# A decoder layer on one core: high weights times high and low activations in one product of 512 columns

## The chip, the cores and the metric

The kernel runs on one core of one Trainium2 chip. The metric is the device time of one execution in microseconds (us); lower is better. The engines are named as in the profile: PE is TensorE (PEld its loads of weights), DVE is VectorE, ACT is ScalarE, POOL is GpSimd, SP is SyncE, which issues the large loads.

## The reference

One layer of a decoder on 256 tokens (S), width 2048 (D), all in float32. Cut to what matters:

```
u = RMSNorm(h)
[qkv_A | z_A | b_A | a_A | q_B | k_B | v_B | g_B | gate_A | gate_B] = u @ w_in     # 2048 x 16400
o_A = gated DeltaNet (short causal conv and silu on q, k, v; chunked delta rule)
o_B = multi-scale retention (rotary q, k; fixed decay per head)
h = h + (sigmoid(gate_A) * o_A + sigmoid(gate_B) * o_B) @ w_out                    # 2048 x 2048
h = h + (silu(hn @ w_gate) * (hn @ w_up)) @ w_down,   hn = RMSNorm(h)              # inner width 5632
return RMSNorm(h)
```

Some 300 MB of weights are read once, each time against 256 tokens.

## The kernel before, in words

**Three passes.** Every product with weights is made of three: each weight tile is rounded to a high part (ScalarE, line 163) and the rest is its low part (VectorE, line 164). The activations are kept in the same two parts, `uh`, `ul` in the first phase, `m` (high and low halves) for the output projection, `hh`, `hl` and `fh`, `fl` behind it. Summed are high weights by high activations (L229), high weights by low activations (L230), and low weights by high activations (L232).

**Units.** The work on weights is a row of units of up to 1 MB. `run_units` takes them one after the other: it emits the load of a unit ahead (SP, L150), the split of a unit ahead, the unit's products, and then what reads the sums (events, `after`). There are three kinds:

- feature-major units (`feature_major`): one tile of 128 output features. The weights are the stationary operand, 128 x 128 for each k-tile, and the 256 tokens of an activation tile move past them. The sums take 256 of the 512 columns of one PSUM bank. With 16 k-tiles that is 48 products of 256 columns; the units of the down projection have 11 k-tiles, so 33. They serve q, k, v of both mixers (`conv_unit`, `rot_evac`; tiles ps_k, ps_q, ps_v, ps_r), the output projection (ps_wo), gate and up (ps_wg, ps_wu) and down (ps_wd).
- token-major units (`token_major`; tiles ps_t): activations stationary, weights moving, 24 products of 512 columns.
- units of Strassen's products (`strassen`; tiles pst_t, pst_sg, pst_su): 21 products of 256 columns of a pair of k-tiles, after VectorE has made three sums of the raw weights (L181 to L183).

**Order.** The first phase (projections and mixers, four blocks of two heads) is ordered by the framework's scheduler on every engine. In the second phase (output projection, gate, up, down) Strassen's units are spread among the others (`FPOS`), and from the 30th unit on (`MAN0`) VectorE keeps the order of the program: split of the unit two ahead, then what reads the sums of the unit before. The other engines stay with the scheduler. Every engine works its own queue in order. High and low parts have two buffers each in the first phase and three in the second, so a split two units ahead waits until TensorE has left a buffer.

**Readers of the sums.** `conv_unit` reads the bank once (L461), `rot_evac` three times (L758 to L760), `wo_evac` (L1071) and `down_ev` (L1176) once, adding to the residual hT; `gate_ev` (L1155) and `up_ev` (L1166) once, multiplying by the norm.

Of the kernel before, what the change touches and what calls it, by code (L numbers as in the profile page):

```python
# [12 lines left out]
P = 128  # L13
# [19 lines left out]
# and where: after which unit of their block, among how many units  # L33
# [15 lines left out]
# buffers; units split ahead in the two phases; units loaded ahead of that  # L49
# [14 lines left out]
def kernel(  # L64
# [15 lines left out]
    # the banks of Strassen's sums serve the units and the mixers as well while there are none  # L80
# [74 lines left out]
    split_ins = {}  # unit -> the last instructions of its split, on ScalarE and VectorE  # L155
# [11 lines left out]
    def load_next(pieces=1):  # L167
        """emit the next unit's split into high and low parts, and its load if that hasn't been"""
# [16 lines left out]
    def after(n, fn):  # L185
        """emit fn after the products of n more units"""
        events.setdefault(done[0] + n, []).append(fn)

    def chain(gen):
        """emit the steps of gen one by one, one after each unit"""  # L190
# [30 lines left out]
    def feature_major(src, nk, ah, al, name, evac):  # L221
        o = []

        def begin():
            o.append(ps_unit(f"ps_{name}")[:, :S])

        def products(hi, lo, k0, k1):
            for k in range(k0, k1):
                PE.matmul(o[0], hi[:, k * P:(k + 1) * P], ah[:, k, :], start=(k == 0), stop=False)  # L229
                PE.matmul(o[0], hi[:, k * P:(k + 1) * P], al[:, k, :], start=False, stop=False)  # L230
            for k in range(k0, k1):
                PE.matmul(o[0], lo[:, k * P:(k + 1) * P], ah[:, k, :], start=False, stop=(k == nk - 1))  # L232
# [10 lines left out]
    def start_pair(before):  # L243
        """the first two units, loaded and computed by quarters in turn, each after what `before` emits"""
# [48 lines left out]
    # -- Strassen's products on one block of 512 columns, token-major --  # L293
    def strassen(src, x, zt, name, then, before=None):
# [3 lines left out]
        def lhs(h):  # L298
# [5 lines left out]
            # product: its token operand, slot of its weights, bank and half of its sum  # L304
# [1046 lines left out]
```

## Time and profile before

| | |
|---|---|
| times of three runs | 1665.67, 1666.42, 1667.9 us; median 1666.42 us |
| span of the profiled execution, first to last instruction | 1664.6 us |
| TensorE | busy 1640.4 us, 13210 products, mean granted clock 0.995 of full speed |
| VectorE | busy 1267.8 us (76%) |
| ScalarE | busy 808.6 us (49%) |
| HBM | 297.27 MB read, 180 GB/s over the span |

The profiled execution is one of the program on the chip; its span leaves out what lies before the first and behind the last instruction, 1.8 us against the median. The records of products overlap (each shows some 160 ns longer than its turn takes), so their pitch, from start to start, is the number to read, not their duration.

### The profile page before, as it was taken

To read this page: it belongs to the slowest core of one execution; us is meant where nothing else is said; L and a number is where in the kernel's file an instruction comes from. 1 tells how busy PE (TensorE), PEld (TensorE's weight loads), DVE (VectorE), ACT (ScalarE), POOL (GpSimd) and SP (SyncE) were. 2 spreads that over 40 slices of the span, in tenths; PEclk is the share of its full clock that TensorE was granted. 3 is DMA by queue.
4 is the path that set the end of the run, shared out by engine and by line. 5 is a ranking of instruction groups with operands and counts; after the bars stand their busy time and mean duration, and the time that the engine had idled before them with its cause. 6 is when DMAs were issued, how large, how long until landed. Compare 5 with 4: busy or idle time off the path is not lost.

```text
span 1664.6 us, 30825 instructions
## 1 busy us (share of the span) xinstructions
PE 1640.4 (99%) x13210; PEld 1558.5 (94%) x13210; DVE 1267.8 (76%) x1719; ACT 808.6 (49%) x850; POOL 28.7 (2%) x63
## 2 busy tenths in 40 slices
PE   7999999999999999999999999999999999999997
PEld 6987899988998889988899999999999999999997
DVE  7797468887888878776675757788778888788754
ACT  5664444445544545445465434444444445354443
POOL 0000000000000000000000000000000000000000
PEclk9999999999999999999999999999999999999998
DMA  7544453454635555344675445465545656466552
GB/s 268 177 153 174 155 194 127 168 185 170 213 131 179 185 180 194 132 168 157 232 270 182 178 152 178 146 219 203 193 170 183 205 190 226 143 205 212 177 181 86
DMA packets 55721, 301.36 MB, mean 181 GB/s; under 512 B 6816, under 2 KB 7072, under 8 KB 32672
## 3 DMA queue, kind: packets, MB, share of 16 engines
q1 hardware_dynamic: 54144, 295.31, 51.4%
q10 hardware_dynamic: 1440, 4.08, 0.7%
q8 instruction: 103, 1.69, 0.4%
q14 instruction: 34, 0.28, 0.0%
HBM read 297.27 MB, written 2.10 MB: 180 GB/s over the span
## 4 chain that ended last, share of the span: by engine, by line
PE 52%; issue 44%; DMA 2%; DVE 2%; ACT 0%; SPq 0%; POOLq 0%; POOL 0%; DVEq 0%; ACTq 0%
PE ps_t L280 7%; PE ps_t L285 7%; PE ps_t L281 7%; PE pst_t L322 6%; PE ps_v L230 2%; PE ps_v L229 2%; PE ps_r L229 2%; PE ps_v L232 2%; PE ps_r L230 2%; PE ps_r L232 2%; PE ps_wo L229 2%; PE ps_wo L230 2%; PE ps_wo L232 1%; PE ps_q L232 1%; PE ps_q L230 1%
## 5 line engine op out<-in xcount | busy, mean ns | idle before, releaser
L163 ACT ACTIVATE hi_t<-raw_t 128x2048 fp32r<-128x2048 f32 (+1 forms) x100 | 183.1, 1832 | 203.7 <-PE ps_t L281 99.2
L164 DVE TENSOR_TENSOR lo_t<-raw_t,hi_t 128x2048 fp32r<-128x2048 f32 (+1 forms) x100 | 217.8, 2182 | 62.4 <-ACT hi_t L163 42.4
L280 PE MATMUL ps_t<-hi_t,uh 128*128 128x512 f32 x480 | 190.7, 397 | 0.5 <-DVE gs L834 0.5
L281 PE MATMUL ps_t<-hi_t,ul 128*128 128x512 f32 x480 | 188.6, 393 | 0.0
L229 PE MATMUL ps_wd<-fh,hi_wd 128*128 128x256 f32 x704 | 169.3, 281 | 1.0 <-DVE fl L1143 1.0
L230 PE MATMUL ps_wd<-fl,hi_wd 128*128 128x256 f32 x704 | 169.6, 281 | 0.0
L229 PEld LDWEIGHTS ps_wd<-fh,hi_wd 128*128 128x128 f32 x704 | 132.8, 189 | 1.2 <-DVE fl L1143 1.2
L230 PEld LDWEIGHTS ps_wd<-fl,hi_wd 128*128 128x128 f32 x704 | 132.9, 189 | 0.0
L163 ACT ACTIVATE hi_wd<-raw_wd 128x1408 fp32r<-128x1408 f32 x64 | 88.4, 1381 | 86.7 <-PE ps_wd L230 35.0
L285 PE MATMUL ps_t<-lo_t,uh 128*128 128x512 f32 x480 | 123.5, 395 | 0.0
L229 PE MATMUL ps_wu<-hh,hi_wu 128*128 128x256 f32 x448 | 109.2, 282 | 0.0
L230 PE MATMUL ps_wu<-hl,hi_wu 128*128 128x256 f32 x448 | 109.1, 283 | 0.0
L230 PE MATMUL ps_wg<-hl,hi_wg 128*128 128x256 f32 x448 | 108.9, 283 | 0.0
L229 PE MATMUL ps_wg<-hh,hi_wg 128*128 128x256 f32 x448 | 108.9, 282 | 0.0
L164 DVE TENSOR_TENSOR lo_wd<-raw_wd,hi_wd 128x1408 fp32r<-128x1408 f32 x64 | 103.6, 1620 | 6.6 <-ACT hi_wd L163 6.5
L280 PEld LDWEIGHTS ps_t<-hi_t,uh 128*128 128x128 f32 x480 | 90.2, 188 | 19.1 <-PE pst_t L322 0.9
L281 PEld LDWEIGHTS ps_t<-hi_t,ul 128*128 128x128 f32 x480 | 90.2, 188 | 17.7
L285 PEld LDWEIGHTS ps_t<-lo_t,uh 128*128 128x128 f32 x480 | 88.9, 188 | 18.1
L232 PE MATMUL ps_wd<-fh,lo_wd 128*128 128x256 f32 x704 | 93.6, 281 | 0.0
L163 ACT ACTIVATE hi_sg<-raw_sg 128x1792 fp32r<-128x1792 f32 x32 | 54.5, 1704 | 71.9 <-DVE raw_sg L183 24.1
L232 PEld LDWEIGHTS ps_wd<-fh,lo_wd 128*128 128x128 f32 x704 | 87.8, 189 | 0.0
L229 PEld LDWEIGHTS ps_wg<-hh,hi_wg 128*128 128x128 f32 x448 | 85.4, 191 | 0.0
(361 smaller groups left out, 4092.1 us busy)
## 6 DMA issues: line engine op xcount, KB each, us to landing
raw_t<-in_wtm_dram SPq DMA_DIRECT2D x60, 1024.0 KB, 4.8
raw_wd<-in_wdown_dram SPq DMA_DIRECT2D x64, 704.0 KB, 4.1
raw_wg<-in_wgate_dram SPq DMA_DIRECT2D x28, 1024.0 KB, 4.8
raw_wu<-in_wup_dram SPq DMA_DIRECT2D x28, 1024.0 KB, 4.8
raw_t<-in_wsm_dram SPq DMA_DIRECT2D x40, 512.0 KB, 3.3
raw_v<-in_wqk_dram SPq DMA_DIRECT2D x16, 1024.0 KB, 4.7
raw_r<-in_wqk_dram SPq DMA_DIRECT2D x16, 1024.0 KB, 4.8
raw_wo<-in_wout_dram SPq DMA_DIRECT2D x16, 1024.0 KB, 4.8
```

Source lines behind the costliest of these rows:

```text
L163: ia = A_.activation(hi[:, r], w[:, r], AF.Copy)
L164: iv = V.tensor_tensor(out=lo[:, r], in0=w[:, r], in1=hi[:, r].bitcast(F32), op=ALU.subtract)
L229: PE.matmul(o[0], hi[:, k * P:(k + 1) * P], ah[:, k, :], start=(k == 0), stop=False)
L230: PE.matmul(o[0], hi[:, k * P:(k + 1) * P], al[:, k, :], start=False, stop=False)
L232: PE.matmul(o[0], lo[:, k * P:(k + 1) * P], ah[:, k, :], start=False, stop=(k == nk - 1))
L280: PE.matmul(pst[c], uh[:, k, c * P:(c + 1) * P], w, start=(k == 0), stop=False)
L281: PE.matmul(pst[c], ul[:, k, c * P:(c + 1) * P], w, start=False, stop=False)
L285: PE.matmul(pst[c], uh[:, k, c * P:(c + 1) * P], lo[:, j * 512:(j + 1) * 512], start=False, stop=(k == KT - 1))
L322: PE.matmul(T[bank][:, half * S:(half + 1) * S], op(j), w[:, slot * 256:(slot + 1) * 256], start=(j == 0 and w is hi and h and half == 0), ...
```

## The change

The two parts of every activation that feature-major units use now lie side by side: `u2`, `h2`, `f2` and `m` are [128, k, 2, 256], and the old names are views of them. For a high weight tile one product of 512 columns takes the place of two of 256: high by high into the first half of the bank, high by low into the second. Low weights by high activations stay products of 256 columns into the first half. The two halves of the bank are added by those who read them.

```diff
         def begin():
-            o.append(ps_unit(f"ps_{name}")[:, :S])
+            o.append(ps_unit(f"ps_{name}"))
 
         def products(hi, lo, k0, k1):
             for k in range(k0, k1):
-                PE.matmul(o[0], hi[:, k * P:(k + 1) * P], ah[:, k, :], start=(k == 0), stop=False)
-                PE.matmul(o[0], hi[:, k * P:(k + 1) * P], al[:, k, :], start=False, stop=False)
+                PE.matmul(o[0], hi[:, k * P:(k + 1) * P], flat(a[:, k]), start=(k == 0), stop=(k == nk - 1),
+                          skip_group_check=True)
             for k in range(k0, k1):
-                PE.matmul(o[0], lo[:, k * P:(k + 1) * P], ah[:, k, :], start=False, stop=(k == nk - 1))
+                PE.matmul(o[0][:, :S], lo[:, k * P:(k + 1) * P], a[:, k, 0], start=False, stop=(k == nk - 1),
+                          skip_group_check=True)
...
-    uh = act.tile([P, KT, S], F32R, tag="a0", name="uh")
-    ul = act.tile([P, KT, S], F32R, tag="a1", name="ul")
+    u2 = act.tile([P, KT, 2, S], F32R, tag="a0", name="u2")
+    uh, ul = u2[:, :, 0], u2[:, :, 1]
...
-            V.tensor_tensor(out=cb[:, 3:], in0=o, in1=rstd_b, op=ALU.mult)
+            cl = t1(f"cl_{name}")
+            A_.activation(cl, o[:, S:], AF.Copy)
+            V.tensor_tensor(out=cl, in0=o[:, :S], in1=cl, op=ALU.add)
+            V.tensor_tensor(out=cb[:, 3:], in0=cl, in1=rstd_b, op=ALU.mult)
...
-            def evac(o):
+            def evac(ps):
+                o = t1(f"ro_{b}_{i}")
+                A_.activation(o, ps[:, S:], AF.Copy)
+                V.tensor_tensor(out=o, in0=ps[:, :S], in1=o, op=ALU.add)
...
-                V.tensor_tensor(out=hT[:, f], in0=o, in1=hT[:, f], op=ALU.add)
+                for i in range(2):
+                    V.tensor_tensor(out=hT[:, f], in0=o[:, i * S:(i + 1) * S], in1=hT[:, f], op=ALU.add)
...
+        def whole(o, name):
+
+            t = t1(name)
+            A_.activation(t, o[:, S:], AF.Copy)
+            V.tensor_tensor(out=t, in0=o[:, :S], in1=t, op=ALU.add)
+            return t
...
-                gs = pend[f] = t1(f"gs{f}")
-                V.tensor_tensor(out=gs, in0=o, in1=rb2, op=ALU.mult)
+                gs = pend[f] = whole(o, f"gs{f}")
+                V.tensor_tensor(out=gs, in0=gs, in1=rb2, op=ALU.mult)
...
-                us = t1(f"us{f}")
-                V.tensor_tensor(out=us, in0=o, in1=rb2, op=ALU.mult)
+                us = whole(o, f"us{f}")
+                V.tensor_tensor(out=us, in0=us, in1=rb2, op=ALU.mult)
```

The edit of hT is in `wo_evac` and `down_ev` alike. The scheduler orders the changed program anew. Three places show how.

**VectorE, among the first down units** (lo_wd and ps_wd are units of the down projection, raw_su, lo_su and Z_sg, sg_g belong to Strassen's units). Before:

```order
L1176 TENSOR_TENSOR hT<-ps_wd_1_10963,hT 128x256
L1112 SCALAR_TENSOR_TENSOR sg_g_11034<-Z_sg_11027,rt_8323,sg_g_11034 128x512
L164 TENSOR_TENSOR lo_su_0_11041<-raw_su_0_10997,hi_su_0_11040 128x1792
L181 TENSOR_TENSOR raw_su_1_11078<-raw_su_1_11078 128x512
L182 TENSOR_TENSOR raw_su_1_11078<-raw_su_1_11078 128x256
L183 TENSOR_TENSOR raw_su_1_11078<-raw_su_1_11078 128x256
L164 TENSOR_TENSOR lo_wd_4_11084<-raw_wd_4_11038,hi_wd_4_11083 128x1408
```

Now:

```order
L1194 TENSOR_TENSOR hT<-ps_wd_1_9778,hT 128x256 x2
L1129 SCALAR_TENSOR_TENSOR sg_g_9838<-Z_sg_9831,rt_7697,sg_g_9838 128x512
L164 TENSOR_TENSOR lo_su_0_9846<-raw_su_0_9801,hi_su_0_9845 128x1792
L181 TENSOR_TENSOR raw_su_1_9872<-raw_su_1_9872 128x512
L182 TENSOR_TENSOR raw_su_1_9872<-raw_su_1_9872 128x256
L183 TENSOR_TENSOR raw_su_1_9872<-raw_su_1_9872 128x256
L164 TENSOR_TENSOR lo_wd_4_9878<-raw_wd_4_9843,hi_wd_4_9877 128x1408
```

The order stands; each reading of the sums has become two instructions, ahead of the next splits.

**TensorE, at the ends of two down units of the same stretch.** Before:

```order
L229 MATMUL ps_wd_8_11418<-fh_9521,hi_wd_8_11343 128x256
L230 MATMUL ps_wd_8_11418<-fl_9522,hi_wd_8_11343 128x256
L232 MATMUL ps_wd_8_11418<-fh_9521,lo_wd_8_11344 128x256 x11
L322 MATMUL pst_su_2_11132<-hi_su_4_11371,hh 128x256
L322 MATMUL pst_su_0_11130<-hi_su_4_11371,hh 128x256
```

Now:

```order
L231 MATMUL ps_wd_8_10162<-f_8609,hi_wd_8_10097 128x512 x10
L234 MATMUL ps_wd_7_10130<-f_8609,lo_wd_7_10066 128x256 x11
L231 MATMUL ps_wd_8_10162<-f_8609,hi_wd_8_10097 128x512
L231 MATMUL ps_wd_9_10225<-f_8609,hi_wd_9_10158 128x512 x7
L234 MATMUL ps_wd_8_10162<-f_8609,lo_wd_8_10098 128x256 x11
L328 MATMUL pst_su_2_9916<-hi_su_4_10126,h_7693 128x256
```

The products with low weights have moved back, behind high products of the next unit. The program before has such places too, but far fewer.

**ScalarE, at gate and up units of the second part** (hi_wg, hi_wu, hi_sg are splits; gs, us the new copies). Before:

```order
L163 ACTIVATE hi_wg_12012<-raw_wg_11975 128x2048
L1157 ACTIVATE sg_12004<-gs_12002 128x256
L163 ACTIVATE hi_sg_3_12067<-raw_sg_3_12007 128x1792
L163 ACTIVATE hi_wu_12102<-raw_wu_12065 128x2048
L1168 ACTIVATE fh_11959<-us_12092 128x256
```

Now:

```order
L163 ACTIVATE hi_sg_2_10625<-raw_sg_2_10566 128x1792
L1174 ACTIVATE sg_10654<-gs_10650 128x256
L1104 ACTIVATE us_10726<-ps_wu_10666 128x256
L163 ACTIVATE hi_wu_10738<-raw_wu_10699 128x2048
L163 ACTIVATE hi_sg_3_10701<-raw_sg_3_10657 128x1792
L1185 ACTIVATE f_10608<-us_10726 128x256
```

The copy of the second half (L1104) stands ahead of the two splits that are issued next, and those wait behind it.

## Rows read from the trace of the kernel before

**Rows 1.** The page: busy time by engine, and TensorE's granted clock in 40 slices.
```profile
PE 1640.4 (99%) x13210; PEld 1558.5 (94%) x13210; DVE 1267.8 (76%) x1719; ACT 808.6 (49%) x850; POOL 28.7 (2%) x63
...
PEclk9999999999999999999999999999999999999998
```

**Rows 2.** Waits of TensorE, first and last of 11: us in total, times, longest.
```profile
PE ss_n L946 <- DVE sx L942: 3.9, 2, 3.2
...
PE ps_wo L229 <- ACT hi_wo L163: 0.3, 1, 0.3
```

**Rows 3.** Timeline of TensorE in one output-projection unit: start, duration, instruction.
```profile
902.05 0.28 PE L229 MATMUL ps_wo<-m,hi_wo 128*128 128x256 f32 x1
...
905.89 2.07 PE L232 MATMUL ps_wo<-m,lo_wo 128*128 128x256 f32 x16
```

**Rows 4.** Timeline of TensorE, token-major units: mid-stream, and behind products of 256 columns.
```profile
341.46 0.39 PE L280 MATMUL ps_t<-hi_t,uh 128*128 128x512 f32 x1
...
345.09 1.97 PE L285 MATMUL ps_t<-lo_t,uh 128*128 128x512 f32 x8
...
512.50 0.40 PE L280 MATMUL ps_t<-hi_t,uh 128*128 128x512 f32 x1
...
513.43 0.39 PE L280 MATMUL ps_t<-hi_t,uh 128*128 128x512 f32 x1
...
515.02 0.39 PE L281 MATMUL ps_t<-hi_t,ul 128*128 128x512 f32 x1
...
516.15 0.59 PE L771 MATMUL psc<-rot 128*128 128x256 f32 x2
```

**Rows 5.** Groups of TensorE by line and shape: busy us, mean ns, idle before.
```profile
L229 PE MATMUL ps_wd<-fh,hi_wd 128*128 128x256 f32 x704 | 169.3, 281 | 1.0 <-DVE fl L1143 1.0
...
L229 PE MATMUL ps_wu<-hh,hi_wu 128*128 128x256 f32 x448 | 109.2, 282 | 0.0
...
L229 PE MATMUL ps_v<-uh,hi_v 128*128 128x256 f32 x256 | 63.6, 286 | 0.6 <-DVE cb_v L461 0.6
...
L229 PE MATMUL ps_k<-uh,hi_k 128*128 128x256 f32 x128 | 31.6, 286 | 1.8 <-ACT hi_k L163 1.8
```

**Rows 6.** Groups of VectorE by line and shape.
```profile
L1176 DVE TENSOR_TENSOR hT<-ps_wd,hT 128x256 f32<-128x256 f32 x64 | 26.8, 418 | 5.4 <-PE ps_wd L232 5.4
```

**Rows 7.** Groups of ScalarE by line and shape.
```profile
L163 ACT ACTIVATE hi_wu<-raw_wu 128x2048 fp32r<-128x2048 f32 x28 | 53.6, 1915 | 43.9 <-PE pst_sg L322 10.7 <-PE pst_su L322 7.7 <-issue 7.7
...
L336 ACT ACTIVATE s_sg<-pst_sg 128x256 f32<-128x256 f32 x4 | 1.5, 366 | 0.0
```

**Rows 8.** Busy time in stretches: PE, PEld, DVE, ACT, POOL, clock, DMA share, GB/s.
```profile
20.00:30.00 10.00, 4.40 (x33) 3.45 (x35) 8.83 (x6) 5.04 (x6) 0.00 (x0) 0.81 0.70 267
...
460.00:510.00 50.00, 49.44 (x606) 47.96 (x604) 44.48 (x79) 23.52 (x29) 1.56 (x5) 1.00 0.44 145
860.00:900.00 40.00, 40.00 (x335) 40.00 (x335) 26.00 (x35) 21.54 (x27) 0.00 (x0) 1.00 0.52 185
1060.00:1100.00 40.00, 40.00 (x340) 40.00 (x340) 33.44 (x39) 19.03 (x15) 0.00 (x0) 1.00 0.59 187
```

**Rows 9.** Waits of VectorE from 1060 to 1100 us, the two longest of five.
```profile
DVE lo_su L164 <- ACT hi_su L163: 2.8, 3, 1.6
DVE Z_sg L338 <- ACT s_sg L336: 1.9, 1, 1.9
```

**Rows 10.** Timeline of VectorE and TensorE in that stretch.
```profile
1085.70 1.62 DVE L164 TENSOR_TENSOR lo_wd<-raw_wd,hi_wd 128x1408 fp32r<-128x1408 f32 x1
...
1088.48 1.48 PE L232 MATMUL ps_wd<-fh,lo_wd 128*128 128x256 f32 x11
```

**Rows 11.** Timeline at the end of the span.
```profile
1651.49 0.42 DVE L1176 TENSOR_TENSOR hT<-ps_wd,hT 128x256 f32<-128x256 f32 x1 [2.54 <-PE ps_wd L232]
```

**Rows 12.** All waits of VectorE, by who was waited for.
```profile
DVE fl L1169 <- ACT fh L1168: 25.4, 27, 4.3
...
DVE gs L1158 <- ACT sg L1157: 19.9, 22, 2.0
```

More of the change, by code (lines that the diff above doesn't have):

```diff
@@ L219, in flush, with feature_major @@
                 fn()
-    def feature_major(src, nk, ah, al, name, evac):
+    def feature_major(src, nk, a, name, evac):
         o = []
         def begin():
-            o.append(ps_unit(f"ps_{name}")[:, :S])
+            o.append(ps_unit(f"ps_{name}"))
         def products(hi, lo, k0, k1):
             for k in range(k0, k1):
-                PE.matmul(o[0], hi[:, k * P:(k + 1) * P], ah[:, k, :], start=(k == 0), stop=False)
-                PE.matmul(o[0], hi[:, k * P:(k + 1) * P], al[:, k, :], start=False, stop=False)
+                PE.matmul(o[0], hi[:, k * P:(k + 1) * P], flat(a[:, k]), start=(k == 0), stop=(k == nk - 1),
+                          skip_group_check=True)
             for k in range(k0, k1):
-                PE.matmul(o[0], lo[:, k * P:(k + 1) * P], ah[:, k, :], start=False, stop=(k == nk - 1))
+                PE.matmul(o[0][:, :S], lo[:, k * P:(k + 1) * P], a[:, k, 0], start=False, stop=(k == nk - 1),
+                          skip_group_check=True)
         def compute(hi, lo):
@@ L291, in token_major, with flat @@
             units.append((src[kg], 2048, f"{name}_{kg}", part(kg)))
+    def flat(t):
+        return t.rearrange("p a b -> p (a b)")
     def strassen(src, x, zt, name, then, before=None):
@@ L439, in z_tiles @@
         return mt([P, 5, S], "Z", f"Z_{name}"), t1(f"s1_{name}")
-    def flat(t):
-        return t.rearrange("p a b -> p (a b)")
     def v4(ps, n=P):
@@ L472, in finish @@
             then(d)
-        feature_major(wqk[b * 12 + i], KT, uh, ul, name, evac)
+        feature_major(wqk[b * 12 + i], KT, u2, name, evac)
     def new_parts(i):
-        mm[i] = act.tile([P, 2, KT // 2, S], F32R, tag=f"a{2 + i}", name=f"m{i}")
+        mm[i] = act.tile([P, KT // 2, 2, S], F32R, tag=f"a{2 + i}", name=f"m{i}")
     def merged_parts(b, j):
         k = 4 * (b % 2) + 2 * j
-        return flat(mm[b // 2][:, 0, k:k + 2]), flat(mm[b // 2][:, 1, k:k + 2])
+        return mm[b // 2][:, k:k + 2, 0], mm[b // 2][:, k:k + 2, 1]
     class Merged:
-        def __init__(self, part):
-            self.part = part
         def __getitem__(self, r):
-            _, k, t = r
-            return mm[k // (KT // 2)][:, self.part, k % (KT // 2), t]
+            k = r[1]
+            return mm[k // (KT // 2)][(r[0], k % (KT // 2)) + r[2:]]
     def split_rest():
@@ L496, in split_rest @@
                 hv, lv = merged_parts(2, j)
-                w = mm["wait"][:, 512 * j:512 * j + 512]
+                w = halves(mm["wait"][:, 512 * j:512 * j + 512])
                 A_.activation(hv, w, AF.Copy)
@@ L864, in merge @@
             hv, lv = merged_parts(b, j)
-            A_.activation(hv, ps, AF.Copy)
-            V.tensor_tensor(out=lv, in0=ps, in1=hv.bitcast(F32), op=ALU.subtract)
+            A_.activation(hv, halves(ps), AF.Copy)
+            V.tensor_tensor(out=lv, in0=halves(ps), in1=hv.bitcast(F32), op=ALU.subtract)
         n = f"{b}"
@@ L877, in block @@
         for i in range(4):
-            feature_major(wqk[b * 12 + 8 + i], KT, uh, ul, f"r{i}" + n, rot_evac(i))
+            feature_major(wqk[b * 12 + 8 + i], KT, u2, f"r{i}" + n, rot_evac(i))
         sides = []
@@ L1014 @@
     first[0] = False
-    mh, ml = Merged(0), Merged(1)
+    merged = Merged()
     with tc.tile_pool(name="ffn", bufs=1) as ffn:
@@ L1028 @@
         nc.scalar.dma_start(wfs, wf)
-        hh = act.tile([P, KT, S], F32R, tag="a0", name="hh")
-        hl = act.tile([P, KT, S], F32R, tag="a1", name="hl")
+        h2 = act.tile([P, KT, 2, S], F32R, tag="a0", name="h2")
+        hh, hl = h2[:, :, 0], h2[:, :, 1]
         sh = act.tile([P, KT // 2, 4, P], F32R, tag="a2", name="sh")
@@ L1089, in sums_of_h, with two @@
                 yield
+        def two(t):
+            return t.rearrange("p (a b) -> p a b", a=2)
+        def whole(o, name):
[3 more added lines that the diff above has]
+            return t
         def z_tiles(name):
@@ L1099, in get_f @@
                 k0, k1, _ = PARTS[pi]
-                fhl[pi] = [ffn.tile([P, k1 - k0, S], F32R, tag=t, name=f"{t}{pi}") for t in ("fh", "fl")]
-            return fhl[pi]
+                fhl[pi] = ffn.tile([P, k1 - k0, 2, S], F32R, tag="f2", name=f"f2{pi}")
+            return fhl[pi][:, :, 0], fhl[pi][:, :, 1]
         def strassen_group(pi, g):
@@ L1141, in turn @@
                     j = g - PARTS[pi][0] + 2 * m
-                    A_.activation(flat(fh[:, j:j + 2]), ps, AF.Copy)
-                    V.tensor_tensor(out=flat(fl[:, j:j + 2]), in0=ps, in1=flat(fh[:, j:j + 2]).bitcast(F32),
+                    A_.activation(fh[:, j:j + 2], two(ps), AF.Copy)
+                    V.tensor_tensor(out=fl[:, j:j + 2], in0=two(ps), in1=fh[:, j:j + 2].bitcast(F32),
                                     op=ALU.subtract)
@@ L1175, in run @@
             def run(o):
-                V.tensor_tensor(out=hT[:, f], in0=o, in1=hT[:, f], op=ALU.add)
+                for i in range(2):
+                    V.tensor_tensor(out=hT[:, f], in0=o[:, i * S:(i + 1) * S], in1=hT[:, f], op=ALU.add)
                 if last:
@@ L1196 @@
         for f in range(KT):
-            feature_major(wout[f], KT, mh, ml, f"wo{f}", wo_evac(f))
+            feature_major(wout[f], KT, merged, f"wo{f}", wo_evac(f))
         def plain(pi):
@@ L1202, in plain @@
                 i = STD.index(f)
-                feature_major(wgate[i], KT, hh, hl, f"wg{f}", gate_ev(f))
-                feature_major(wup[i], KT, hh, hl, f"wu{f}", up_ev(pi, f))
+                feature_major(wgate[i], KT, h2, f"wg{f}", gate_ev(f))
+                feature_major(wup[i], KT, h2, f"wu{f}", up_ev(pi, f))
         def down(pi):
@@ L1211, in late, with __init__ @@
                     n = len(units)
-                    feature_major(wdown[f, :, k0 * P:k1 * P], k1 - k0, Late(pi, 0), Late(pi, 1), f"wd{pi}_{f}",
-                                  down_ev(pi, f))
+                    feature_major(wdown[f, :, k0 * P:k1 * P], k1 - k0, Late(pi), f"wd{pi}_{f}", down_ev(pi, f))
                 late()
         class Late:
-            def __init__(self, pi, i):
-                self.pi, self.i = pi, i
+            def __init__(self, pi):
+                self.pi = pi
             def __getitem__(self, r):
-                return fhl[self.pi][self.i][r]
+                return fhl[self.pi][r]
         def strassen_groups(pi):
```

## The prediction

> **What bounds the kernel now.** The page first [rows 1]: TensorE is busy 1640.4 of 1664.6 us, and its granted clock reads full speed (the 2.4 GHz level) in every slice but the last. Busy time alone proves little here, because the records of products overlap, so I read two other things. The waits of TensorE: the longest of eleven kinds is 3.9 us at the start, the last 0.3 us [rows 2], so it hardly ever stands still. And its pitch: in a unit of the output projection 32 products go from 902.05 to 905.89 us, 0.120 us each, with nothing between them [rows 3]. So the span is TensorE's row of products, and only their number and pitch count, as long as the other engines deliver. VectorE, at 76%, is next [rows 1].
>
> **What the change takes away.** The kernel already has products of 512 columns, in its token-major units, so the new pitch need not be guessed: 16 of them mid-stream take 345.09 - 341.46 = 3.63 us, 0.227 each [rows 4]. Two of 256 take 0.240. The second 256 columns thus cost 0.107, and the 0.013 left of a 256-wide product's 0.120 are a fixed part, which a pair then pays once instead of twice. Pairs: L229 has 704 for down, 448 for up and as many for gate, 256 each for v, r and the output projection, 128 each for k and q [rows 5], 2624 in all. At the steady pitch that is 2624 x 0.013 = 34.1 us. But the first 512-wide products behind 256-wide ones are slower: four from 512.50 to 513.43 take 0.2325 each [rows 4], and every unit now goes from 256 to 512. So I count by units: 16 from 512.50 to 516.15 take 3.65 us against 3.84 [rows 3, 4], 0.19 saved; 11, to 515.02, take 2.52 against 22 x 0.120 = 2.64, 0.12 saved. 120 units x 0.19 + 64 down units x 0.12 = **30.5 us**. Bounds: 34.1 from the steady pitch; 19.7 if every product ran at 0.2325 (2624 x 0.0075).
>
> One page speaks against that fixed part. The Trainium skill ("TensorE: Matmul & The Clock Gate", Back-to-back issue gap) gives a warm pitch of N/2.4 + 2.5 ns: a pair would then save 2.5 ns, 6.6 us in all. This trace has 120 and 227 ns where that rule gives 109 and 216, so by the trace the fixed part is five times as large.
>
> **What it adds.** Each of the 184 feature-major units gets one more VectorE instruction of 128 x 256, an add in line with L1176, 0.418 us [rows 6]: 77 us. The 48 units of the first phase and the 56 of gate and up also get a copy on ScalarE, as L336 copies from PSUM in 0.366 us [rows 7]: 38 us, on an engine busy 49% [rows 1]. No DMA is added and SyncE's order does not change. PSUM banks, buffers and the sizes of the splits stay. Strided views of the activations cost nothing that I can see: the pieces are still 256 long.
>
> **What hides VectorE's 77 us, and where not.** From 860 to 900 us VectorE is busy 26.0 of 40 us [rows 8]; seven adds of 0.42 vanish there. From 1060 to 1100, down units among Strassen's, it is busy 33.4 [rows 8] and loses 4.7 more in its two longest waits for ScalarE [rows 9]; the list of its waits there names TensorE not once, so no idle time stems from being ahead. What protects TensorE is only the distance between split and use: the low part that ends at 1085.70 + 1.62 = 1087.32 is used at 1088.48 [rows 10], 1.16 us later, the shortest in the second phase. Some six adds (2.5 us) and a TensorE earlier by six times 0.12 us make VectorE 3.2 us later against it in this stretch, so 2 us would be waited. Of the 14 stretches of 40 us from 1020 to 1580 I count six as tight: 12 us. This is softened: in the new order the products with low weights stand behind high products of the next unit, which puts the use of a low part off by up to 11 x 0.227 = 2.5 us. That is about the size of the shortage, but it also asks for the next high part earlier, and the adds that read the bank come later by as much. I take half, **6 us**. In the first phase blocks 1 to 3 have such a stretch each (460 to 510: VectorE 44.5 of 50 [rows 8]); seven adds of 0.42 and a TensorE earlier by 7 x 0.19 make 4.3 us against 5.5 us idle, part of it waits that stay. I take 2 us for each, **6 us**, since the scheduler's new order there moves the readers too. Bounds for both together: 0, if the order and the buffers absorb all, and 2 x 14 + 4.3 x 3 = 41 us, if every stretch were like the tight one and no reserve helped.
>
> **The ends.** In the first 30 us TensorE waits for loads and splits (busy 4.4 of 10 from 20 to 30 [rows 8]), so the first three units save nothing: 3 x 0.19 = 0.6 us back. At the end the last down unit is read by one VectorE add at 1651.49 with everything else behind it [rows 11]; a second adds 0.4 us.
>
> **Sum.** 1664.6 - 30.5 + 6 + 6 + 0.6 + 0.4 = 1647.1 us of span. The median of the runs lies 1.8 us over the profiled span, so 1648.9; I forecast **1649 us**, 1.0% faster. What this kernel's measurement can tell from no change is about 0.2%, 3.3 us: faster is below 1663.1, slower above 1669.7.
>
> **The rivals.**
>
> *All hidden.* VectorE's adds cost 3 us or less, and the pitch is nearly the steady one: 1666.4 - 30.5 to 33 + 1 to 4 = 1634 to 1640. For it: ScalarE and VectorE have 30 to 50% idle on the whole, and the order on TensorE has been moved to wait for low parts later. Against: the stretch from 1060 to 1100 has no idle time left to fill. Chance 0.23.
>
> *The fixed part is not saved.* A 512-wide product between loads of weights for 256-wide ones might pay it twice over, so that a pair keeps nearly its old 0.240 us. The nearest row is the first of such a run, 0.2325 on average over four, and as it is at 0.227 from the fifth on [rows 4], little speaks for it. Saved would be 2624 x 2.5 ns or so, 7 us, less 6 us of waits: 1665, in the band of no change. The Trainium skill's page named above would have a saving of that size, by its small fixed part, and the trace does not agree. Chance 0.06.
>
> *VectorE becomes the bound (slower).* It works in order, and the add of gate and up waits for the copy on ScalarE. If that copy stands behind a split, VectorE stands too, up to 1.9 us [rows 7], and with it all splits queued behind. An up unit with a Strassen unit costs VectorE 2.3 + 2.0 + 1.5 (sums of raw weights) + 3 x 0.42 = 7.1 us and its wait for fh some 0.9 (25.4 / 28 [rows 12]), 8.0 in all; for gate the wait for sg is 0.7 (19.9 / 28 [rows 12]). TensorE needs 48 x 0.120 + 21 x 0.120 = 8.28 before and 8.09 after. With the add VectorE is at 8.4 already; with half a split of waiting, 0.95, at 9.4. Some 40 of the 56 gate and up units lie among Strassen's: 40 x (9.4 - 8.28) = 45 us, less what the rest saves (16 x 0.19 + 64 x 0.12 + 64 x 0.19 = 23): 1688. From 40 x (0.12 + wait) = 23 it is no longer faster from a wait of 0.46 us per copy on. Against it: in the order on ScalarE the copy stands ahead of the two splits that follow, and what it waits for, the products, is done a unit earlier. Chance 0.10, of which 0.08 lie above 1669.7.
>
> *Forecast.* Partly paid back, 1640 to 1659: 0.61.
>
> **How the numbers follow.** Faster: 0.61 + 0.23 + 0.02 of the others = 0.86. Same: 0.06. Slower: 0.08. The range leaves out the slower rival and the part of "all hidden" below 1636, together about 0.2: 1636 to 1663, which also holds the loss of 12 us grown to twice its size. The forecast's own range is 1640 to 1659.
>
> **What the profile after would show.** L231 would read x2624 less missing records, at a pitch of 0.227 to 0.2285 inside a unit; a unit of the output projection would take 5.55 us instead of 5.76 from start to start, at the same granted clock. VectorE's busy time would be near 1345 us, ScalarE's near 847. The list of TensorE's waits would have grown by some 10 us, on low parts (L164) in the stretches between 1060 and 1540 and on readers of PSUM or merged parts in the first phase. The whole L1105 would seldom wait for L1104 longer than 0.5 us. I am wrong if the pitch of a 512-wide product among 256-wide ones is above 0.232, or if TensorE's new waits are beyond 20 us, or if they are near zero.

## The result and the profile after

The changed kernel takes **1708.8 us** (median of 4 runs, 1706.4 to 1709.3) where the one before takes 1666.5: a ratio of 1.0249, 95% interval 1.0235 to 1.0264. It is 42 us slower, where 1649 us and a gain were forecast.

The page of the kernel after, to be held against [rows 1]: busy time and TensorE's granted clock.

```profile
PE 1641.4 (96%) x10586; PEld 1437.5 (84%) x10586; DVE 1342.7 (79%) x1903; ACT 833.0 (49%) x953; POOL 28.3 (2%) x63
...
PEclk9899999999989999999999999999999999999998
```

There are 2624 products fewer, as there should be, and VectorE's busy time is 1342.7 us (1345 forecast). But TensorE's share has fallen from 99% to 96%, and its clock dips in slices of the first half. (A digit of 9 stands for anything from 0.90 on: the 0.81 of [rows 8] lies in a slice that reads 9.) Waits of TensorE, us in total, times, longest [rows 2]:

```profile
PE pv L748 <- DVE vt L477: 9.8, 3, 4.0
PE pss_k L530 <- DVE kT L477: 5.6, 2, 2.9
PE pv L748 <- DVE sse_q L536: 4.7, 1, 4.7
PE ss_n L952 <- DVE sx L948: 4.0, 2, 3.2
PE ps_v L231 <- DVE cl_k L466: 3.2, 1, 3.2
...
PE pss_q L530 <- DVE sse_k L536: 2.9, 1, 2.9
...
PE ps_wd L234 <- DVE lo_wd L164: 2.7, 3, 1.4
```

Before, only two waits in the first 30 us were longer than 2 us. Now there are nine of 2.8 to 4.7 us behind them in the first phase, and seven of the nine are transposes of q, k and v (pss, pv) that wait for the end of the readers' chains. The boundary between the phases is the first product of the output projection. It starts at 819.86 us before and here:

```profile
865.95 2.37 PE L231 MATMUL ps_wo<-m,hi_wo 128*128 128x512 f32 x9 [0.76 <-ACT gs L838]
```

So the first phase lost 46 us and the second gained 3 (from there to the end 841.5 us, before 844.8). (The expectations give 818.7 and 864.8 for the two starts, a slip of mine of about 1.2 us in both; the difference is the same.)

**One wait, step by step.** The timeline of all engines (start, duration, instruction; in brackets the idle time ahead of it and what ended it):

```profile
291.01 0.28 PE L328 MATMUL pst_t<-lo_t,ush 128*128 128x256 f32 x1
291.25 1.91 ACT L163 ACTIVATE hi_r<-raw_r 128x2048 fp32r<-128x2048 f32 x1 [2.20 <-PE pst_t L328]
293.07 0.40 ACT L475 ACTIVATE sg_v<-cv_v 128x256 f32<-128x256 f32 x1
293.19 2.29 DVE L164 TENSOR_TENSOR lo_r<-raw_r,hi_r 128x2048 fp32r<-128x2048 f32 x1 [1.48 <-ACT hi_r L163]
...
295.40 0.42 DVE L477 TENSOR_TENSOR vt<-cv_v,sg_v 128x256 f32<-128x256 f32 x1
...
295.97 0.66 PE L748 MATMUL pv<-cs,vt 128*128 128x128 f32 x2 [4.68 <-DVE sse_q L536]
```

ScalarE stood 2.20 us at the split `hi_r`, whose buffer TensorE left only at 291.3. The sigmoid of the readers' chain stands behind it, and `vt` stands behind the low part `lo_r` on VectorE. TensorE's transposes wait for `vt`, and so does the next work that would free a buffer: 4.68 us in which three engines wait in turn for each other. (The releaser named, sse_q, ended just before; the products of the group take `vt`.)

**The wait is paid again in the clock.** Stretches behind that wait: PE, PEld, DVE, ACT, POOL busy, granted clock, DMA share, GB/s.

```profile
291.00:296.00 5.00, 0.32 (x4) 0.14 (x2) 3.49 (x6) 3.52 (x11) 0.12 (x2) 0.81 0.06 23
296.00:300.00 4.00, 4.00 (x41) 3.02 (x42) 2.93 (x9) 0.51 (x1) 1.04 (x2) 0.50 0.40 131
300.00:304.00 4.00, 4.00 (x24) 3.48 (x22) 3.20 (x9) 2.34 (x4) 0.10 (x1) 0.88 0.00 0
304.00:308.00 4.00, 4.00 (x53) 3.35 (x52) 3.30 (x6) 1.91 (x5) 0.00 (x0) 1.00 0.01 4
```

After the standstill the granted clock is 0.50, the 1.2 GHz level, for 4 us, then 0.88: 4 x 0.50 + 4 x 0.12 = 2.5 us more, half of this wait again.

### The profile page after: what moved, and what is told of

Same layout as the page of the kernel before. It is cut to its first block, busy times and chain, and to the rows that moved or that the text cites. A ratio compares the mean times of both kernels' runs of the same rounds, so it can differ in the third digit from the quotient of the medians.

```text
span 1707.5 us, 25893 instructions
## 1 busy us (share of the span) xinstructions
PE 1641.4 (96%) x10586; PEld 1437.5 (84%) x10586; DVE 1342.7 (79%) x1903; ACT 833.0 (49%) x953; POOL 28.3 (2%) x63
## 4 chain that ended last, share of the span: by engine, by line
PE 50%; issue 44%; DVE 4%; DMA 1%; ACT 1%; SPq 0%; DVEq 0%; POOLq 0%; POOL 0%; ACTq 0%
PE ps_t L283 7%; PE ps_t L288 6%; PE ps_t L284 6%; PE pst_t L328 5%; PE ps_r L231 4%; PE ps_wo L231 3%; PE ps_v L231 3%; PE ps_wo L234 2%; PE ps_q L231 2%; PE ps_r L234 2%; PE ps_v L234 1%; PE ps_k L231 1%; DVE lo_t L164 1%; PE ps_q L234 1%; DVE lo_v L164 1%
## 5 line engine op out<-in xcount | busy, mean ns | idle before, releaser
L283 PE MATMUL ps_t<-hi_t,u 128*128 128x512 f32 x480 | 191.4, 399 | 0.5 <-DVE gs L840 0.5
L284 PE MATMUL ps_t<-hi_t,u 128*128 128x512 f32 x480 | 188.1, 392 | 0.0
L231 PE MATMUL ps_wd<-f,hi_wd 128*128 128x512 f32 x704 | 175.5, 395 | 1.6 <-DVE f L1160 1.6
L231 PEld LDWEIGHTS ps_wd<-f,hi_wd 128*128 128x128 f32 x704 | 127.8, 188 | 26.8 <-DVE f L1160 1.8
L163 ACT ACTIVATE hi_wd<-raw_wd 128x1408 fp32r<-128x1408 f32 x64 | 87.8, 1378 | 103.3 <-DMA raw_wd<-in_wdown_dram 34.5
L288 PE MATMUL ps_t<-lo_t,u 128*128 128x512 f32 x480 | 123.2, 394 | 0.0
L231 PE MATMUL ps_wg<-h,hi_wg 128*128 128x512 f32 x448 | 109.8, 393 | 1.7 <-ACT hi_wg L163 1.7
L231 PE MATMUL ps_wu<-h,hi_wu 128*128 128x512 f32 x448 | 108.4, 392 | 0.0
L283 PEld LDWEIGHTS ps_t<-hi_t,u 128*128 128x128 f32 x480 | 90.2, 188 | 19.2 <-PE pst_t L328 0.9
L284 PEld LDWEIGHTS ps_t<-hi_t,u 128*128 128x128 f32 x480 | 90.2, 188 | 17.8
L288 PEld LDWEIGHTS ps_t<-lo_t,u 128*128 128x128 f32 x480 | 89.1, 188 | 18.1
L234 PEld LDWEIGHTS ps_wd<-f,lo_wd 128*128 128x128 f32 x704 | 91.3, 189 | 7.9 <-DVE lo_wd L164 3.5
L234 PE MATMUL ps_wd<-f,lo_wd 128*128 128x256 f32 x704 | 93.9, 281 | 2.7 <-DVE lo_wd L164 2.7
L164 DVE TENSOR_TENSOR lo_su<-raw_su,hi_su 128x1792 fp32r<-128x1792 f32 x32 | 64.7, 2022 | 10.7 <-ACT hi_su L163 10.7
L163 ACT ACTIVATE hi_wg<-raw_wg 128x2048 fp32r<-128x2048 f32 x28 | 53.6, 1914 | 39.8 <-PE ps_wu L231 15.3
```

Source lines behind the costliest of these rows:

```text
L163: ia = A_.activation(hi[:, r], w[:, r], AF.Copy)
L164: iv = V.tensor_tensor(out=lo[:, r], in0=w[:, r], in1=hi[:, r].bitcast(F32), op=ALU.subtract)
L231: PE.matmul(o[0], hi[:, k * P:(k + 1) * P], flat(a[:, k]), start=(k == 0), stop=(k == nk - 1), skip_group_check=True)
L234: PE.matmul(o[0][:, :S], lo[:, k * P:(k + 1) * P], a[:, k, 0], start=False, stop=(k == nk - 1), skip_group_check=True)
L283: PE.matmul(pst[c], uh[:, k, c * P:(c + 1) * P], w, start=(k == 0), stop=False)
L284: PE.matmul(pst[c], ul[:, k, c * P:(c + 1) * P], w, start=False, stop=False)
```

## The experiments

Besides medians, each run gives three numbers from its trace: the start of the first `ps_wo` (end of the first phase), the rest of the span, and the sum of TensorE's gaps over 0.1 us from 30 us to the first `ps_wo`. Ratios are against the kernel before on the same chip; each interval is about +-0.0015. The profiled execution can lie a little off the median (e5's is 2.2 us below it, e18's 1.6 above).

| run | median | ratio | first ps_wo | rest | gaps |
|---|---|---|---|---|---|
| before | 1666.5 | | 819.9 | 844.8 | 1.1 |
| after | 1708.8 | 1.0249 | 865.9 | 841.5 | 34.7 |
| e1 second phase only | 1663.3 | 0.9982 | 819.2 | 842.2 | 1.1 |
| e2 first phase only | 1711.2 | 1.0265 | 865.8 | 843.7 | 34.7 |
| e3 old pairs, new readers | 1724.9 | 1.0349 | 873.9 | 850.3 | 34.5 |
| e4 new products, old readers | 1655.7 | 0.9937 | 824.1 | 830.9 | 7.3 |
| e5 before, with a copy | 1693.0 | 1.0163 | 844.5 | 844.2 | 21.5 |
| e6 before, with an add | 1690.5 | 1.0143 | 844.7 | 844.2 | 18.2 |
| e7 no copy | 1691.7 | 1.0153 | 848.5 | 841.7 | 25.9 |
| e8 add on GpSimd | 1692.6 | 1.0161 | 852.7 | 837.9 | 29.2 |
| e9 one unit later | 1710.7 | 1.0269 | 867.8 | 840.9 | 39.6 |
| e10 before, one unit later | 1671.4 | 1.0032 | 824.4 | 844.3 | 5.3 |
| e11 second phase, no down | 1658.2 | 0.9952 | 819.9 | 836.4 | 1.1 |
| e12 the same, last down part | 1658.3 | 0.9953 | 820.1 | 836.1 | 1.1 |
| e13 readers first | 1714.1 | 1.0289 | 869.5 | 842.0 | 38.0 |
| e14 readers first, no copy | 1690.4 | 1.0152 | 846.3 | 841.9 | 22.2 |
| e15 before, add, readers first | 1688.8 | 1.0140 | 843.9 | 844.4 | 15.3 |
| e16 e13 with e11's second phase | 1707.7 | 1.0252 | 870.1 | 836.2 | 39.8 |
| e17 half the low parts | 1664.2 | 0.9987 | 821.0 | 841.9 | 7.1 |
| e18 low quarter on GpSimd | 1695.7 | 1.0175 | 854.0 | 841.6 | 26.5 |

**Which phase, and products or readers (e1 to e4).**

```diff
+        wide = not first[0]                # e1; first[0] in e2; False in e3
...
+                if wide: ...               # one product of 512 columns
+                PE.matmul(o[0][:, :S], hi[...], a[:, k, 0], ...)
+                PE.matmul(o[0][:, :S], hi[...], a[:, k, 1], ...)    # e3: into o[0][:, S:]
...
-            cl = t1(f"cl_{name}")              # the old readers again: e1 in the first phase, e2 in the second, e4 in both
-            A_.activation(cl, o[:, S:], AF.Copy)
-            V.tensor_tensor(out=cl, in0=o[:, :S], in1=cl, op=ALU.add)
-            V.tensor_tensor(out=cb[:, 3:], in0=cl, in1=rstd_b, op=ALU.mult)
+            V.tensor_tensor(out=cb[:, 3:], in0=o[:, :S], in1=rstd_b, op=ALU.mult)
...
```

> Only the second phase has the products of 512 columns and the new readers; the first phase has the old pairs of 256 and the old readers, on the new side-by-side layout. The first products of ps_wo come at 818.7 us before and 864.8 us after, so the changed kernel loses 46 us ahead of the second phase and gains 3 in it. Theory (the readers of the first phase lose it): 1666.5 - 3 = 1663, with the first products of ps_wo at 818 to 820. Rival (the layout with strides of two halves makes every use of uh and ul slower): the first phase still loses, 1680 or more.

> Only the first phase has the products of 512 columns and the new readers; the second is as before. Theory: 1666.5 + 46 = 1712, first products of ps_wo at 864 to 866. Rival (part of what is seen at the end of the first phase is paid back because the second one starts with a fuller set of loaded weights): 1700 or less.

> Products stay pairs of 256 columns, but high by low goes into the second half of the bank, and all readers are the new ones. Theory (the readers and the order that comes of them lose the time): TensorE saves nothing and the first phase loses at least what it lost, so its end is near 818.7 + 46 + 9 = 874 us or somewhat less, the whole 1700 to 1735. Rival (the faster products run into splits that come too late, and the readers cost nothing): no loss, 1665 to 1672.

> Products of 512 columns everywhere, but the old readers, which read the first half alone: the sums of high weights by low activations are formed and left out. Theory: TensorE's saving of 30 us comes out nearly whole, 1636 to 1642, the first phase ends 9 us earlier, near 810. Rival (faster products run into late splits): the first phase still loses 20 us or more, 1680 to 1705.

e1 and e2 came out as expected by the theory: the two phases add up, and the strided layout costs nothing. e3 shows that the new readers alone cost 54 us in the first phase (873.9 - 819.9). e4 missed its forecast of 1636 to 1642: with the faster products alone the first phase still ends 4.2 us later than before, not 9 earlier. It too has the waits for q's chain, though fewer, in the order that the scheduler makes for it (TensorE's waits in e4):

```profile
PE pP L598 <- DVE Mc L590: 3.2, 1, 3.2
...
PE pss_q L527 <- DVE qT L474: 1.8, 1, 1.8
PE pq L721 <- DVE qT L474: 1.8, 1, 1.8
```

**Copy or add (e5 to e8).**

```diff
+            A_.activation(cl, o, AF.Copy)                                # e5, before the norm's product
...
+            V.tensor_tensor(out=cl, in0=o, in1=rstd_b, op=ALU.mult)      # e6
+            V.tensor_tensor(out=cb[:, 3:], in0=cl, in1=cl, op=ALU.max)
...
+            V.tensor_tensor(out=cl, in0=o[:, :S], in1=rstd_b, op=ALU.mult)           # e7
+            V.tensor_tensor(out=cb[:, 3:], in0=o[:, S:], in1=rstd_b, op=ALU.mult)
+            V.tensor_tensor(out=cb[:, 3:], in0=cb[:, 3:], in1=cl, op=ALU.add)
...
+            A_.activation(cv, o[:, :S], AF.Copy)                         # e8, after cl's copy
+            G.tensor_tensor(out=cl, in0=cv, in1=cl, op=ALU.add)
```

> The kernel before, but in the first phase each of the 48 units of q, k, v is first copied out of PSUM by ScalarE, and the old readers take the copy: one more crossing to ScalarE and back, no more work on VectorE, the old products. Theory A (the longer chain of readers, one more crossing of two queues in order): the first phase loses about as much as with all new readers, some 40 to 54 us, 1705 to 1720. Theory B (VectorE's added work): little, 1666 to 1675.

> The kernel before, but in the first phase each of the 48 units has one more VectorE instruction of 128 x 256 in the chain of its readers, and no copy on ScalarE; the old products. Theory A (crossings): little, 1666 to 1675. Theory B (VectorE's added work, or the order that the scheduler makes of it): 1695 to 1720.

> The changed kernel, but in the first phase VectorE alone adds the halves: each half times the norm, then the sum, so one crossing to ScalarE less and one VectorE instruction more per unit of q, k, v of the delta rule (one more for retention in place of the copy). Theory A: much of the loss comes back, 1670 to 1690. Theory B: it grows or stays, 1705 to 1725.

> The changed kernel, but in the first phase ScalarE copies both halves and GpSimd adds them, so VectorE has the work that it had before, and the chain of readers is longer by a copy and a step on GpSimd. Theory A: the loss stays or grows, 1705 to 1730. Theory B: most of it comes back, 1665 to 1685.

All four times fell between the ranges of the two theories. By itself the copy costs 24.6 us of the first phase (844.5), the add 24.8 (844.7), together about the 54 of e3; e7 (one more VectorE step in place of the copy) and e8 (one more copy and a step on GpSimd in place of the add) give back 13 to 17. Each step is, with its handover, some 0.4 to 0.5 us long and comes 48 times, which makes 20 to 24. But that is no price per step, and that the sums agree is luck, as the four blocks show (below, behind e18).

**The distance (e9, e10).**

```diff
-W_AT0, W_AT, W_TR0, W_TR = 6, 1, 5, 1
+W_AT0, W_AT, W_TR0, W_TR = 7, 2, 6, 2
...
-                    after(2 if b == 0 and h == 0 else 1, lambda: v_tokens(h))
+                    after(3 if b == 0 and h == 0 else 2, lambda: v_tokens(h))
```

> The changed kernel, but in the first phase TensorE's transposes and products that follow q, k and v come one unit later than they did (two units after the products, where it was one). Theory C (a readers' chain that has grown by a copy and an add no longer ends within the one unit between a unit's products and the transposes of its result, which TensorE reaches in order): the first phase ends near 815 to 830 us in place of 866, the whole 1657 to 1675. Rival (ScalarE and VectorE can't do the chains and the splits at this pace, whatever the distance): the waits move and stay, 1695 or more.

> The kernel before with the same shift by one unit, no other change: the price of the shift. It has no waits there to take away. Theory C: 1663 to 1675. Rival (the mixers' own chain, triangle to merge, then ends too late): 1680 or more.

Theory C fell: e9 keeps the whole loss (the shift alone makes the first phase of the kernel before 4.6 us longer, and e10 is within its range). The transposes stand later on TensorE, and the chains end later by as much (TensorE's waits in e9):

```profile
PE pv L748 <- DVE vt L477: 10.7, 4, 3.1
PE pss_q L530 <- DVE qT L477: 7.3, 2, 4.0
PE pss_k L530 <- DVE kT L477: 6.4, 2, 3.6
```

**The order of the queues (e13 to e16).** The split of a unit is put behind the readers' chain of the q, k or v unit three before.

```diff
+            for ins in read_ins.get(i - 3, ()):          # that unit's sigmoid, and its last product on VectorE
+                st.enter_context(tc.issue_after(ins))
+            split_part(i, slice(0, n))
```

> The changed kernel, but in the first phase the split of a unit stands on ScalarE and on VectorE behind the readers' chain of the q, k or v unit three before it. Theory E (the order: steps of the chain stand behind splits that can't start): TensorE's waits of some 34 us in the first phase and the slower clock behind them, 20 us, mostly go; it ends near 815 to 830 us in place of 866, the whole 1657 to 1675. Rival (the work itself is too much at this pace): 1695 or more.

> The same order, with VectorE alone adding the halves in the first phase (1691.7 without the new order). Theory E: 1655 to 1672; against the run before it, one crossing less and 0.42 us more of VectorE in each chain, within 8 us. Rival: 1685 or more.

> The kernel before with one more VectorE instruction in each chain of the first phase (1690.5 without the new order), in the same order of splits and readers. Theory E: 1664 to 1675. Rival: 1685 or more.

> The first phase of the first of these runs, and the change in the output projection, gate and up, with the old down projection. By theory E: the first run's time less 5 us, 1652 to 1670; if the order does nothing, 1695 to 1705. It beats the version that has the change in the second phase alone without down (1658.2) if the first phase ends before 820 us.

Theory E fell as well, in all four: each came out at its rival's time, or above it. In block 2 of e13 the sigmoid `sg_v` now starts at 512.19 us, ahead of the split `hi_r` at 512.51, and TensorE still waits 2.90 us for `vt`; other waits have moved to the splits that now stand behind the chains (TensorE's waits in e13):

```profile
PE ps_v L240 <- ACT hi_v L163: 11.3, 8, 5.4
PE pss_q L544 <- DVE qT L490: 6.1, 3, 3.5
PE pv L762 <- DVE vt L490: 6.1, 6, 2.9
PE ps_r L240 <- ACT hi_r L163: 4.1, 6, 0.9
```

The sum of the gaps hardly changes, 38.0 us for 34.7. That one order and the other cost the same suggests that too much stands in the queues; it doesn't show it.

**VectorE's own time (e17, e18).** Between the first v and the first r unit of block 1 VectorE of the kernel before is busy 25.91 of 29.3 us:

```profile
249.00:278.30 29.30, 29.30 (x327) 28.57 (x326) 25.91 (x54) 13.79 (x29) 2.48 (x6) 1.00 0.33 109
```

and these are all its waits there, 3.1 us together, none of them for TensorE:

```profile
DVE lo_r L164 <- ACT hi_r L163: 1.3, 1, 1.3
DVE raw_t L181 <- DMA raw_t<-in_wsm_dram: 1.0, 1, 1.0
DVE vt L471 <- ACT sg_v L469: 0.5, 1, 0.5
DVE cb_q L461 <- ACT jn_k L530: 0.3, 1, 0.3
```

Counting its waits, 29.0 of 29.3 us are taken, although VectorE is busy only 88%. (In block 2, from 444.7 to 476.7 us, 1.8 us of its waits are for TensorE.) That VectorE has no time left there is a reading, and e6 speaks against taking it literally: one more VectorE step in each unit makes this block 1.3 us longer.

```diff
+        if first[0] and i > 2 and name[0] in "kqvr":
+            r = slice(0, 1024)                           # e17; low products of k >= 8 take tile k - 8
...
+            p = slice(1536, 2048)                        # e18
+            G.tensor_tensor(out=lo[:, p], in0=w[:, p], in1=hi[:, p].bitcast(F32), op=ALU.subtract)
+            r = slice(0, 1536)
```

> The changed kernel, but from the fourth unit on VectorE makes the low part of only 8 of 16 k-tiles for each q, k, v and r unit; the low products of the other 8 take the same tiles again, so the true low part of half the weights of those units is left out and TensorE's work stays. VectorE has 1.14 us less in each of these units, and the change had added 0.42 and a wait for a copy of about as much. Theory F (VectorE, busy or in its in-order waits for ScalarE, bounds the stretches of q, k, v): nearly all of the loss of the first phase goes, it ends at 810 to 820 us, the whole 1652 to 1664. Rival (the length of the readers' chain by itself): 1695 or more.

> The changed kernel, but GpSimd makes the last quarter of the low part (128 x 512) of each q, k, v and r unit of the first phase; nothing is left out. VectorE has 0.57 us less in each, against 0.42 and a wait of about as much added. GpSimd took 1.4 to 1.9 us for 128 x 256, so about 3 us for each quarter, within a unit of 5.55. Theory F: half to two thirds of the loss comes back, 1670 to 1690, if GpSimd's own small steps behind these quarters and the later end of the low part cost no more than a few us. Rival: 1700 or more.

e17 ends its first phase at 820.99 us. The loss, counted from where the saved products alone would have brought it (below, 812.4), was 53.5 us; 45 of them are back, with 1.07 us less on VectorE per unit (2290 ns for a low part, now 1224). That is over twice the add that the change had brought, the low parts are ready sooner, and TensorE's order of units has changed back in part of the phase (next paragraphs). e18 gave back only 12 and missed its forecast. GpSimd took 2.2 us for each quarter, and those of VectorE's instructions with both inputs in SBUF that ran beside it became slower. Groups of VectorE from 30 to 800 us, first of the kernel after, then of e18:

```profile
L477 DVE TENSOR_TENSOR vt<-cv_v,sg_v 128x256 f32<-128x256 f32 x16 | 6.7, 421 | 2.8 <-ACT sg_v L475 2.8
```

```profile
L481 DVE TENSOR_TENSOR vt<-cv_v,sg_v 128x256 f32<-128x256 f32 x16 | 12.0, 749 | 4.1 <-ACT sg_v L479 4.1
```

The mean has gone from 421 to 749 ns, at the very end of the chain that TensorE waits for (the median is still 426; the longest takes 1518).

**By block, and an order that no edit asked for.** A block lasts from its first `ps_k` to that of the next one (the last to the first `ps_wo`); us, and for the runs the difference to before:

| run | block 0 | block 1 | block 2 | block 3 | first v ahead of the second q in blocks 2 and 3 |
|---|---|---|---|---|---|
| before | 216.0 | 197.9 | 198.3 | 199.8 | no |
| after | +15.1 | +10.9 | +12.3 | +8.0 | yes |
| e3 both steps, old pairs | +12.6 | +13.6 | +17.1 | +11.1 | yes |
| e4 new products alone | -1.7 | -2.1 | +7.0 | +1.5 | yes |
| e5 copy alone | +10.6 | +0.2 | +7.1 | +6.9 | yes |
| e6 add alone | +8.3 | +1.3 | +8.6 | +7.1 | yes |
| e13 readers first | +13.2 | +10.7 | +16.1 | +9.5 | no |
| e17 half the low parts | -0.7 | +1.4 | +2.7 | -2.2 | no |

In block 1 the copy alone costs 0.2 us and the add alone 1.3, but both together 13.6 (e3): the costs of the steps don't add up within a block, though their sums over the phase nearly do.

The last column is a change that no edit asked for. Before, TensorE takes both q units of a block and then the v units; in ten of the runs, the changed kernel among them, the scheduler puts the first v unit between the two q units in blocks 2 and 3. Block 2 of the changed kernel:

```profile
459.92 3.94 PE L231 MATMUL ps_q<-u,hi_q 128*128 128x512 f32 x16 [1.03 <-DVE cl_k L466]
...
466.40 3.94 PE L231 MATMUL ps_v<-u,hi_v 128*128 128x512 f32 x16
...
475.64 5.23 PE L231 MATMUL ps_q<-u,hi_q 128*128 128x512 f32 x16
```

e4 has this order and no added step: its blocks 0 and 1 gain about the 1.9 us that 192 pairs save, and its blocks 2 and 3 lose. So in blocks 0 and 1, where the order of the units stands, the loss comes of the readers, and there e17 takes away most of it; in blocks 2 and 3 the scheduler's order has a part in it. e13, whose splits are held back, has the old order of units and loses all the same, so the order alone does not explain those blocks either.

**A version that beats both (e11, e12).** The change stays in the output projection and in gate and up; the first phase and the down projection (in e12 all but its last part) are as before.

```diff
+        wide = not first[0] and name[:2] != "wd"         # e12: ... or name[2] == "3"
```

> The change in the output projection and in gate and up alone; the first phase and the down projection as before. The down projection's pairs of 256 take 118.2 + 118.2 ns where one product of 512 takes 232.4, so 704 x 4 ns = 2.8 us of saving go, and with them 64 adds of 0.42 on VectorE. Theory (the second phase's waits, some 8 us more than with the old readers, come from VectorE being late in stretches with down units): against the second phase alone (1663.3) 5 to 8 us of waits go, so 1658 to 1661. Rival (the waits are at gate and up): 1665 to 1667.

> As the one before, with the change in the last part of the down projection too, where no Strassen's units run and VectorE is busy 28 of 40 us: 176 products x 4 ns = 0.7 us less, and 0.4 us more at the end: the same within 0.5 us.

e11 takes 1658.2 us, a ratio of 0.9952 (0.9937 to 0.9967), 8 us faster than the kernel before and 50 faster than the change. Against e1 it gains 5.8 us behind the first `ps_wo`: 64 adds on VectorE were worth more than the down projection's saving. e12 is the same, as expected.

## Why the prediction was wrong, point by point

**What bounds the kernel: half right.** TensorE's row of products is the span of the kernel before. But "VectorE, at 76%, is next" read an average: in the stretch of q, k and v shown above VectorE's work and waits fill 29.0 of 29.3 us, and the page does not show that.

**The products' term: mechanism right, size too large.** Forecast 30.5 us. e4's second phase, which has no reader changed, measures it: 844.8 - 830.9 = 13.9 us, where the working gave 72 x 0.19 + 64 x 0.12 = 21.4. Two durations were off. A run of 512-wide products between 256-wide ones does not settle at 0.227; where the products of a unit follow each other without a break, the mean pitch is 0.2302 (output projection, up), 0.2307 (gate) and 0.2323 us (down), nearer the 0.2325 of its first four [rows 4]. And a pair of the down projection took not 0.240 but 0.2364 us before, as two rows of one unit show (11 products in 1112.94 - 1111.64 = 1.30 us, 0.118 each):

```profile
1111.64 1.47 PE L232 MATMUL ps_wd<-fh,lo_wd 128*128 128x256 f32 x11
1112.94 0.52 PE L322 MATMUL pst_su<-hi_su,hh 128*128 128x256 f32 x3
```

So a down unit saves 0.04 to 0.05 us, not 0.12. At 9.8 ns a pair (0.240 - 0.2302, an estimate from the second phase), 768 pairs give the first phase 7.5 us (9.1 forecast): it would have ended at 812.4. All in all 13.9 + 7.5 = 21.4 us, inside the bounds of the term (19.7 to 34.1), near the lower one. An output projection unit takes 5.64 us from start to start (901.95 - 896.31) for 5.55 forecast and 5.76 before:

```profile
896.31 3.89 PE L231 MATMUL ps_wo<-m,hi_wo 128*128 128x512 f32 x16
...
901.95 3.82 PE L231 MATMUL ps_wo<-m,hi_wo 128*128 128x512 f32 x16
```

**VectorE's lateness in the first phase: the step that failed.** "... seven adds of 0.42 and a TensorE earlier by 7 x 0.19 make 4.3 us against 5.5 us idle, part of it waits that stay. I take 2 us for each": 6 us in all, with a bound of 13. Measured are 865.9 - 812.4 = 53.5 us. Four things are wrong in the step. It counts blocks 1 to 3 and puts block 0 at nothing without a reason, and block 0 lost the most, 15.1 us. The idle time was for the most part taken for a reserve: in the stretch shown above in block 1 all of it, and in that of block 2 over half, was VectorE's waits for ScalarE and DMA. The copy was priced at nothing there ("an engine busy 49%"), but it stands in the chain and by itself costs as much as the add (e5). And the wait was taken at its length: of the 53.5 us, 33.6 are TensorE's gaps (34.7 - 1.1), and the remaining 20 fit the clock, whose mean from 30 to 800 us is 0.97 where it was 1.00 (770 x 0.03 = 23, part of it within the gaps themselves). That price stood in [rows 8], 0.81 in the stretch of the first waits, and was not put into the sum. The bound of 41 us for all waits was set from rows of that same idle time, so it fell with it. The prediction's own sign of being wrong, new waits of TensorE beyond 20 us, came true. What it did foresee, that "the scheduler's new order there moves the readers too", it took as a reason for a smaller figure; e4's blocks 2 and 3 show that a new order can cost.

**VectorE's lateness in the second phase: mechanism right, undersized.** 6 us forecast; e1 against e4 gives 842.2 - 830.9 = 11.3; the largest of TensorE's waits there is for low parts of down units (3.1 us), as foreseen. Most of it comes of the down projection's adds: without them the rest of the span is 836.4 (e11), 2.7 us above 830.9 + 2.8 for the saving that goes with them.

**The ends** (1.0 us): from the last product to the last add of hT are 0.92 us where 0.46 were, the 0.4 us forecast; no run takes out the 0.6 at the start. **The rivals.** The slower one had a mechanism that fits the timeline, VectorE held up in order behind ScalarE's copies and splits, but it was placed at gate and up, where the whole L1105 waits 0.6 us for its copies. It had a chance of 0.10; it should have been worked out for the first phase too, whose chains go to ScalarE and back twice already. That the fixed part is not saved would have meant 2.5 ns a pair; measured are 4.0 (down) to 9.8. The Trainium skill ("TensorE: Matmul & The Clock Gate", Back-to-back issue gap) has the 2.5 ns in a formula that it gives for a product by itself and says not to hold for a stream of loads and products, which the prediction left out. This trace doesn't agree with the 2.5 ns, for down by less than the prediction had it.

**What stays open.** That the added steps of the readers lose the time in blocks 0 and 1 is shown (e4 against after), and e17 shows that shorter low parts on VectorE cure most of it there; e9 and e13 to e16 show that neither that distance nor that order does. Why the steps cost what they do is argued. A copy adds no work to VectorE, and over the phase it costs as much as an add. That it makes VectorE wait in order, as ScalarE's queue is full of splits that wait for buffers, fits the timeline, but no run separated ScalarE's part from VectorE's. e17 also has its low parts ready sooner, and no run tells that apart from the time it leaves VectorE. No run kept the order of TensorE's units fixed, so in blocks 2 and 3 the part of the scheduler's order stays open. A third buffer for high and low parts in the first phase was not tried.

## What to carry to other kernels

Read what an idle engine waits for before you count its idle time as a reserve: waits for a helper in its own chain may stay, and then only a run tells what an added step costs. Price the steps together and stage by stage: in block 1 two steps that cost 0.2 and 1.3 us alone cost 13.6 together. Add to each expected standstill of TensorE what the slower clock takes behind it. Look at the order that the scheduler makes of the changed program, in every experiment too. And a saving of some 10 ns per product, 0.16 us per unit of 16, can be spent by a reader's step of 0.4 us: keep the wide form only in the stages where a run shows that it pays, as e11 does.

## What the runs showed of the hardware

- After a standstill of 4.68 us, the granted clock was 0.50 for 4 us and 0.88 for 4 more, and a 512-wide product took its turn in 0.427 us in the first of these stretches instead of 0.227 to 0.232.
- 512-wide products, each with its own weights, between 256-wide ones have a mean pitch of 0.230 to 0.232 us within the units of the second phase; in token-major units they reach 0.227.
- A VectorE product of 128 x 256 with both inputs in SBUF (`vt`) takes 0.42 us on average in the changed kernel and 0.75 in e18, up to 1.5, where GpSimd works on 128 x 512 in SBUF at times beside it; the sum that reads one input from PSUM stays at 0.416. The Trainium skill ("GPSIMD Engine Reference", 1. Specifications) states that GpSimd shares its SBUF interfaces with VectorE and that VectorE's instructions with two SBUF inputs contend for them; these rows agree.
